# Hybrid decoder block on one core: another order of the second product's seven products, early scaling at its end, and three smaller edits

## The chip, the cores and the metric

The kernel runs on one core of one Trainium2 chip. Its engines are TensorE (PE, matmuls; its weight loads are PEld), VectorE (DVE), ScalarE (ACT), GpSimd (POOL) and SyncE (SP, which issues nearly all transfers). The metric is the device time of one execution in microseconds (us), the median of several.

## The reference

A decoder block over 512 positions of 2048 features, all in float32: eight heads of causal attention with forget gates and eight heads of spatial gating, both from one input projection, an output projection, and a dense layer with squared ReLU between 2048 and 8192 features; a norm ahead of each part and one at the end.

```python
h = rmsnorm(x, norm_mix_g);  z = h @ w_in           # q, k, v, log_f, zu, zv
attn = forgetting_attention(q, k, v, log_sigmoid(z_f + b_f))
gm = chunked_spatial_gating(zu, zv, gmlp_ln_g, gmlp_ln_b, w_s, b_s)
merged = concat(rmsnorm(attn, attn_out_g), rmsnorm(gm, gmlp_out_g))
x = x + merged @ w_out
a = relu(rmsnorm(x, norm_ffn_g) @ w_ff1)
x = x + (a * a) @ w_ff2
return rmsnorm(x, norm_final_g)
```

## The kernel before

Every large product is done with float32 numbers split into a high and a low part: of each tile ScalarE casts the high part (`wh`), VectorE subtracts it for the low part (`wl`), and TensorE does three matmuls (high by high, high by low, low by high). TensorE's instructions stand in the order in which the code is written; those of the other engines are placed by a scheduler, which keeps what their data need.

*Input and output units.* Up to 527 us units of 16 weight tiles make v, qk, zv and zu, with the attention heads' small matmuls between them; the units `oa` (attention's half of the output projection, to 605 us) and `og` (the gated half, to 703 us) follow. Behind each head, ScalarE copies the head's output out of PSUM, POOL squares it and adds the squares up (L429 to L433). The attention's norm `rA` is applied when an `oa` unit ends: VectorE multiplies the PSUM tile by `rA`, POOL adds the block's input `x4` (L600, L601). In `attn_split_task` (L442) the attention's output is cast and split.

*Block sums for the first product.* Beside these units, `sums_task` (L673) loads three blocks of `w_ff1` per step, adds two pairs (L680, L681) and stores both sums, in four steps of the task's clock.

*The first product* (703 to 1353 us) and *the second* (1353 to 1984 us) use seven block products in place of eight. The second has 16 units, eight slices of the hidden features (`kc`) by two halves of the output (`n`). A unit has products P1 to P7, each of two groups (`h`) of 12 matmuls 128x512. The tuple `usual` is the order of the products in a unit; `final` that of the last unit. Four blocks of `w_ff2` (B11, B12, B21, B22) are loaded per unit and half; `prepare` (L880), two groups ahead of the matmuls, forms the block sum that a product needs in place (B11 += B12 for P5, B11 += B22 for P6, B12 += B22 for P7, B21 += B11 beside P6), splits it, and where a block has had its last reader (`follows`) loads the next unit's.

The products accumulate in three pairs of PSUM banks: P1, P6, P7 and P4 in X, P2 in Y, P5 and P3 in Z. P7 goes on in the banks that hold P6, P4 in those of P7; P1, P6 and P5 are copied out by ScalarE when they end (`keep`, L916), and the outputs `acc` add up on VectorE: the PSUM tile (L924, or L909 for P4) and the copy (L925). Unit by unit:

```python
usual = (P1, P2, P5, P6, P7, P3, P4)
final = (P1, P2, P5, P6, P3, P7, P4)
follows = {P6: B11, P7: B12, P3: B22, P4: B21}
```

*The end.* In the last two units (`kc` is `LAST`) each finished output tile is scaled by the second norm's `r2` and added to the residual `x2` (`settle`, L957), and ScalarE squares it with a running sum. `finish` (L961), once per half of the positions, takes the root (`rl`), scales `acc` on VectorE and ScalarE (L972, L970), transposes it on TensorE (L981), multiplies by the last norm's columns, half of each PSUM tile on VectorE and half on ScalarE (L988, L990), and stores 512 KB per piece (L991).

## Time and profile before

| | |
|---|---|
| Median of 3 runs | 2000.34 us (1999.61 to 2003.0) |
| Profiled execution | 2002.97 us, of which the span 2001.3 us |
| Mean granted clock of TensorE | 0.998 |
| TensorE busy | 1966.3 us, 98% |
| VectorE busy | 1597.4 us, 80% |
| ScalarE busy | 1051.7 us, 53% |
| POOL busy | 84.1 us, 4% |
| Mean DMA traffic | 220 GB/s |

The span runs from the first to the last instruction of the profiled execution; the reported time has 1.7 us more around it. Busy time is the union of an engine's instructions. Matmuls overlap and their ends are modelled, so a delay of a fraction of a microsecond need not show as idle time: the distance of the starts tells more. A row of the timeline joins alike instructions that follow one another; "[1.62 <-ACT wh L895]" at its end says that the engine sat idle for 1.62 us before it, until ScalarE's `wh` of line 895 was there.

### The profile page before, as it was taken

To read this page: it belongs to the slowest core of one execution; us is meant where nothing else is said; L and a number is where in the kernel's file an instruction comes from. 1 tells how busy PE (TensorE), PEld (TensorE's weight loads), DVE (VectorE), ACT (ScalarE), POOL (GpSimd) and SP (SyncE) were. 2 spreads that over 40 slices of the span, in tenths; PEclk is the share of its full clock that TensorE was granted. 3 is DMA by queue.
4 is the path that set the end of the run, shared out by engine and by line. 5 is a ranking of instruction groups with operands and counts; after the bars stand their busy time and mean duration, and the time that the engine had idled before them with its cause. 6 is when DMAs were issued, how large, how long until landed. Compare 5 with 4: busy or idle time off the path is not lost.

```text
span 2001.3 us, 30641 instructions
## 1 busy us (share of the span) xinstructions
PE 1966.3 (98%) x11288; PEld 1721.9 (86%) x11288; DVE 1597.4 (80%) x2400; ACT 1051.7 (53%) x1692; POOL 84.1 (4%) x84
## 2 busy tenths in 40 slices
PE   9999999999999999999999999999999999999996
PEld 6888887888787899999999999997888888888875
DVE  7567567677667789888888888888888988998897
ACT  6344334445423566666666666666554444444455
POOL 5000001100121000000000000000000000000000
PEclk9999999999999999999999999999999999999999
DMA  6465565667766789986677667778855656646632
GB/s 217 152 198 167 186 193 174 200 211 242 247 204 199 249 270 307 334 270 201 207 243 238 209 203 236 240 263 314 328 198 202 231 165 224 241 137 237 245 128 84
DMA packets 226406, 439.91 MB, mean 220 GB/s; under 512 B 18896, under 2 KB 96848, under 8 KB 226128
## 3 DMA queue, kind: packets, MB, share of 16 engines
q1 hardware_dynamic: 225568, 436.09, 64.6%
q8 instruction: 88, 1.44, 0.3%
q10 hardware_dynamic: 432, 1.35, 0.2%
q0 software_dynamic: 256, 0.52, 0.1%
q14 instruction: 62, 0.51, 0.1%
HBM read 337.22 MB, written 100.66 MB: 219 GB/s over the span
## 4 chain that ended last, share of the span: by engine, by line
PE 58%; DVE 5%; DMA 3%; issue 1%; ACT 1%; SPq 0%; POOLq 0%; POOL 0%; DVEq 0%; ACTq 0%
PE q L802 28%; PE bX L1078 16%; PE bZ L1078 7%; PE bY L1078 4%; DMA b<-in_w_dram 1%; DVE wl L896 1%; PE ps_og L152 1%; PE ps_og L150 1%; PE ps_og L151 1%; DVE fl L734 1%; DMA x2d<-x2t 1%; DMA x2l<-x2d 0%; DVE acc L957 0%; DVE acc L924 0%; DMA t1d<-b 0%
## 5 line engine op out<-in xcount | busy, mean ns | idle before, releaser
L802 PE MATMUL q<-form,fh 128*128 128x256 f32 x3584 | 647.4, 283 | 1.0 <-DVE x L616 1.0
L802 PEld LDWEIGHTS q<-form,fh 128*128 128x128 f32 x3584 | 559.4, 192 | 1.4 <-DVE x L616 1.0
L802 PE MATMUL q<-form,fl 128*128 128x256 f32 x1792 | 508.6, 284 | 2.1 <-DVE fl L734 1.9
L895 ACT CAST wh<-raw 128x1024 fp32r<-128x1024 f32 x224 | 234.4, 1054 | 221.4 <-PE bX L1078 121.3
L802 PEld LDWEIGHTS q<-form,fl 128*128 128x128 f32 x1792 | 343.9, 192 | 4.1 <-DVE fl L734 3.4
L896 DVE TENSOR_TENSOR wl<-raw,wh 128x1024 fp32r<-128x1024 f32 x224 | 271.2, 1223 | 72.6 <-ACT wh L895 71.7
L1078 PE MATMUL bX<-wh,fac 128*128 128x512 f32 x1008 | 322.3, 393 | 4.3 <-ACT k_wl L916 2.1
L1078 PEld LDWEIGHTS bX<-wh,fac 128*128 128x128 f32 x1008 | 190.0, 188 | 52.3 <-ACT k_wh L916 6.8
L734 DVE TENSOR_TENSOR fl<-t,fh 128x512 fp32r<-128x512 f32 x256 | 176.2, 690 | 68.0 <-ACT fh L733 66.8
L733 ACT CAST fh<-t 128x512 fp32r<-128x512 f32 x256 | 158.2, 618 | 117.0 <-PE q L802 78.8
L1078 PE MATMUL bX<-wl,fac 128*128 128x512 f32 x504 | 198.8, 394 | 1.9 <-DVE wl L896 1.9
L1078 PE MATMUL bZ<-wh,fac 128*128 128x512 f32 x512 | 162.8, 389 | 0.0
L1078 PEld LDWEIGHTS bX<-wl,fac 128*128 128x128 f32 x504 | 95.0, 188 | 25.5 <-DVE wl L896 7.0
L1078 PEld LDWEIGHTS bZ<-wh,fac 128*128 128x128 f32 x512 | 96.1, 188 | 20.0
L733 ACT CAST fh<-r 128x512 fp32r<-128x512 f32 x128 | 79.1, 618 | 46.0 <-PE q L802 39.9
L150 PE MATMUL ps_qk<-xh,wh_qk 128*128 128x512 f32 x256 | 101.6, 397 | 0.0
L152 PE MATMUL ps_qk<-xh,wl_qk 128*128 128x512 f32 x256 | 100.0, 391 | 0.0
L151 PE MATMUL ps_qk<-xl,wh_qk 128*128 128x512 f32 x256 | 99.8, 390 | 0.0
L1078 PE MATMUL bZ<-wl,fac 128*128 128x512 f32 x256 | 99.6, 389 | 0.0
L734 DVE TENSOR_TENSOR fl<-r,fh 128x512 fp32r<-128x512 f32 x128 | 88.2, 689 | 10.1 <-ACT fh L733 9.4
L162 ACT ACTIVATE wh_qk<-raw_qk,cols 128x512 fp32r<-128x512 f32 x64 | 46.3, 724 | 94.7 <-PE ps_qk L151 62.9
L163 DVE SCALAR_TENSOR_TENSOR wl_qk<-raw_qk,cols,wh_qk 128x512 fp32r<-128x512 f32 x64 | 47.7, 750 | 59.0 <-ACT wh_qk L162 58.9
(618 smaller groups left out, 3559.1 us busy)
## 6 DMA issues: line engine op xcount, KB each, us to landing
b<-in_w_dram SPq DMA_DIRECT2D x256, 256.0 KB, 4.4
raw<-in_w_dram SPq DMA_DIRECT2D x128, 512.0 KB, 4.9
fac<-fac SPq DMA_DIRECT2D x112, 512.0 KB, 6.3
r<-in_w_dram SPq DMA_DIRECT2D x64, 512.0 KB, 5.6
fac<-fc SPq DMA_DIRECT2D x48, 512.0 KB, 3.9
raw_qk<-in_win_dram SPq DMA_DIRECT2D x32, 512.0 KB, 3.8
t1d<-b SPq DMA_DIRECT2D x64, 256.0 KB, 2.2
t3d<-b SPq DMA_DIRECT2D x64, 256.0 KB, 2.4
```

Of the source, the lines that this page charges most:

```text
L150: nc.tensor.matmul(ps, lhsT=ah, rhs=bh, start=start, stop=False)
L151: nc.tensor.matmul(ps, lhsT=ah, rhs=bl, start=False, stop=False)
L152: nc.tensor.matmul(ps, lhsT=al, rhs=bh, start=False, stop=stop)
L162: nc.scalar.activation(wh, raw, AF.Copy, scale=g)
L163: nc.vector.scalar_tensor_tensor(wl, raw, g, f(wh), ALU.mult, ALU.subtract)
L733: nc.scalar.copy(pairs(wh), b[p])
L734: nc.vector.tensor_tensor(pairs(wl), b[p], pairs(f(wh)), ALU.subtract)
L802: nc.tensor.matmul(d, lhsT=l[:, c], rhs=r, start=j == 0 and q == 0 and m == 0 and w == 0, stop=j == 3 and q == 1 and w == 2, skip_group_ch ...
L895: nc.scalar.copy(wh, s)
L896: nc.vector.tensor_tensor(wl, s, f(wh), ALU.subtract)
L1078: nc.tensor.matmul(banks[chain][t], lhsT=l, rhs=r, start=start and w == 0, stop=stop and w == 2, skip_group_check=True)
```

## The change

There are five edits.

1. The second product's order becomes P1, P5, P6, P2, P7, P3, P4, so P2 stands between P6 and P7; B21 += B11 moves from P6 to P2, and the next unit's B11 is loaded behind P2.
2. The scaling by `r2` and the residual come early: `settle_task` turns each `acc` into acc * r2 + x2 at the start of the last slice, and the additions of the last two units become scaled additions (`add_scaled`, with `nr2`, the negative of `r2`, for subtractions). Squares have a function of their own; the very last one is VectorE's.
3. In `finish` VectorE scales five of eight tiles and ScalarE three; the transposed tiles use two more PSUM banks, each tile is read by one engine, and the last piece of each half is stored in two parts of 256 KB.
4. `sums_task` does one block sum per step of its clock, with one store behind each.
5. The attention's squares go from POOL to ScalarE; the multiplication by `rA` moves from the end of the `oa` units to `attn_split_task`; the end of an `oa` unit is one addition on VectorE, and POOL's sixteen additions there are gone.

```diff
@@ attention head, split, end of an oa unit
-            nc.gpsimd.tensor_tensor(attnT["ss"], a, a, ALU.mult)
+            nc.scalar.activation(attnT["ss"], a, AF.Square)
...
-            nc.gpsimd.tensor_tensor(sq, a, a, ALU.mult)
+            nc.scalar.activation(sq, a, AF.Square)
             nc.gpsimd.tensor_tensor(attnT["ss"], attnT["ss"], sq, ALU.add)
...
+                nc.vector.tensor_tensor(attnT[c][:, j, :], attnT[c][:, j, :], rA, ALU.mult)
                 nc.scalar.copy(attn_h[c][:, j, :], attnT[c][:, j, :])
...
-                nc.vector.tensor_tensor(o, ps[m], rA, ALU.mult)
-                nc.gpsimd.tensor_tensor(o, o, x4[c][:, m, :], ALU.add)
+                nc.vector.tensor_tensor(o, ps[m], x4[c][:, m, :], ALU.add)
@@ sums_task
                 here(nc.vector.tensor_tensor(b11, b11, b12, ALU.add))
+                yield 1
+                here(nc.sync.dma_start(out=t1d[u][j], in_=b11))
                 here(nc.vector.tensor_tensor(b22, b22, b12, ALU.add))
                 yield 1
-                here(nc.sync.dma_start(out=t1d[u][j], in_=b11))
                 here(nc.sync.dma_start(out=t3d[u][j], in_=b22))
-                yield 1
@@ second product
-    usual = (P1, P2, P5, P6, P7, P3, P4)
+    usual = (P1, P5, P6, P2, P7, P3, P4)
-        final = (P1, P2, P5, P6, P3, P7, P4)
+        final = (P1, P5, P6, P2, P3, P7, P4)
-        follows = {P6: B11, P7: B12, P3: B22, P4: B21}
+        follows = {P2: B11, P7: B12, P3: B22, P4: B21}
...
-            if p == P6:
+            if p == P2:
                 nc.vector.tensor_tensor(raw(B21), raw(B21), raw(B11), ALU.add)
@@ its end
+                if end:
+                    add_scaled(c, t, bank[t], ps_op)
+                    add_scaled(c, t, s[t], s_op)
...
+        def settle_task(n):
+            order = ((0, 2 * n), (0, 2 * n + 1), (1, 2 * n + 1), (1, 2 * n))
+            x2 = {c: load_x2(*c) for c in order}
+            yield 3
+            for c in order:
+                for t in range(2):
+                    a, tb = acc[c][:, t, :], 2 * c[0] + t
+                    nc.vector.scalar_tensor_tensor(a, a, r2[:, tb:tb + 1], x2[c][:, t, :], ALU.mult, ALU.add)
+                yield 1
+
+        def add_scaled(c, t, src, op):
+            a, tb = acc[c][:, t, :], 2 * c[0] + t
+            r = (nr2 if op is ALU.subtract else r2)[:, tb:tb + 1]
+            nc.vector.scalar_tensor_tensor(a, src, r, a, ALU.mult, ALU.add)
...
+            if kc == LAST and p == P1 and h == 0:
+                start_task(settle_task(n))
@@ finish
-                    if t:
+                    if t and q < 3:
                         nc.scalar.activation(a, a, AF.Copy, scale=rt)
...
-                    ps = mm(f"pt{th}{q}{jj}")
+                    i = 2 * q + jj
+                    ps = ax(f"pt{th}{i}", i // 2 % 2) if i % 2 else mm(f"pt{th}{i}")
...
+                    if i in ((1, 2, 4, 6, 7) if th else (0, 2, 4)):
+                        nc.vector.tensor_tensor(d, ps.rearrange("p (j c) -> p j c", j=2),
+                                                cols[:, G_LAST + k:G_LAST + k + 2].unsqueeze(2).broadcast_to([P, 2, 256]),
+                                                ALU.mult)
+                    else:
+                        for j in range(2):
+                            nc.scalar.activation(d[:, j, :], ps[:, j * 256:(j + 1) * 256], AF.Copy,
+                                                 scale=cols[:, G_LAST + k + j:G_LAST + k + j + 1])
+                    if jj or q == 3:
+                        m = slice(0, 4) if q < 3 else slice(2 * jj, 2 * jj + 2)
```

How the change moves the other engines' instructions is seen at three places. ScalarE in unit 6, a steady unit of the second product; `wh6_6_1` is the high part for P6's second half, `k5` the copy of P5, `k2` that of P6, `bX` and `bZ` the PSUM banks. Before:

```order
L895 CAST wh6_5_0_17139<-raw6_0_0_16889 128x1024
L895 CAST wh6_5_1_17158<-raw6_0_1_16911 128x1024
L895 CAST wh6_6_0_17179<-raw6_0_0_16889 128x1024
L916 COPY k5_6_wh_17220<-bZ6_0_17186 128x512
L916 COPY k5_6_wl_17221<-bZ6_1_17187 128x512
L895 CAST wh6_6_1_17201<-raw6_0_1_16911 128x1024
L895 CAST wh6_7_0_17225<-raw6_1_0_16937 128x1024
L895 CAST wh6_7_1_17244<-raw6_1_1_16956 128x1024
L916 COPY k2_6_wh_17262<-bX6_0_17104 128x512
L916 COPY k2_6_wl_17263<-bX6_1_17105 128x512
```

After the change:

```order
L895 CAST wh6_5_0_17094<-raw6_0_0_16883 128x1024
L895 CAST wh6_5_1_17113<-raw6_0_1_16902 128x1024
L916 COPY k1_6_wh_17129<-bX6_0_17098 128x512
L916 COPY k1_6_wl_17130<-bX6_1_17099 128x512
L895 CAST wh6_6_0_17134<-raw6_0_0_16883 128x1024
L895 CAST wh6_6_1_17153<-raw6_0_1_16902 128x1024
L916 COPY k5_6_wh_17169<-bZ6_0_17138 128x512
L916 COPY k5_6_wl_17170<-bZ6_1_17139 128x512
L895 CAST wh6_2_0_17173<-raw6_2_0_17017 128x1024
L895 CAST wh6_2_1_17192<-raw6_2_1_17035 128x1024
L916 COPY k2_6_wh_17211<-bX6_0_17098 128x512
L916 COPY k2_6_wl_17212<-bX6_1_17099 128x512
```

Both casts for P6 now stand ahead of the copies of P5 rather than around them, and the casts for P2 stand between the copies of P5 and those of P6.

VectorE in the same unit, from P5's low part on (`raw6_0` is B11, `raw6_1` B12, `raw6_2` B21, `raw6_3` B22). Before:

```order
L896 TENSOR_TENSOR wl6_5_0_17140<-raw6_0_0_16889,wh6_5_0_17139 128x1024
L889 TENSOR_TENSOR raw6_0_0_16889<-raw6_0_0_16889,raw6_3_0_16981 128x1024
L896 TENSOR_TENSOR wl6_5_1_17159<-raw6_0_1_16911,wh6_5_1_17158 128x1024
L924 TENSOR_TENSOR acc00_15277<-acc00_15277,bY6_0_17143 128x512
L924 TENSOR_TENSOR acc00_15277<-acc00_15277,bY6_1_17144 128x512
L925 TENSOR_TENSOR acc00_15277<-acc00_15277,k1_6_wh_17134 128x512
L925 TENSOR_TENSOR acc00_15277<-acc00_15277,k1_6_wl_17135 128x512
L896 TENSOR_TENSOR wl6_6_0_17180<-raw6_0_0_16889,wh6_6_0_17179 128x1024
L898 TENSOR_TENSOR raw6_2_0_17024<-raw6_2_0_17024,raw6_0_0_16889 128x1024
L889 TENSOR_TENSOR raw6_0_1_16911<-raw6_0_1_16911,raw6_3_1_16999 128x1024
L898 TENSOR_TENSOR raw6_2_1_17042<-raw6_2_1_17042,raw6_0_1_16911 128x1024
L896 TENSOR_TENSOR wl6_6_1_17202<-raw6_0_1_16911,wh6_6_1_17201 128x1024
```

After the change:

```order
L887 TENSOR_TENSOR raw6_0_0_16883<-raw6_0_0_16883,raw6_1_0_16928 128x1024
L896 TENSOR_TENSOR wl6_1_1_17073<-raw6_0_1_16902,wh6_1_1_17072 128x1024
L909 TENSOR_TENSOR acc12_15275<-acc12_15275,bX5_0_16797 128x512
L909 TENSOR_TENSOR acc12_15275<-acc12_15275,bX5_1_16798 128x512
L896 TENSOR_TENSOR wl6_5_0_17095<-raw6_0_0_16883,wh6_5_0_17094 128x1024
L887 TENSOR_TENSOR raw6_0_1_16902<-raw6_0_1_16902,raw6_1_1_16949 128x1024
L889 TENSOR_TENSOR raw6_0_0_16883<-raw6_0_0_16883,raw6_3_0_16974 128x1024
L891 TENSOR_TENSOR raw6_1_0_16928<-raw6_1_0_16928,raw6_3_0_16974 128x1024
L896 TENSOR_TENSOR wl6_5_1_17114<-raw6_0_1_16902,wh6_5_1_17113 128x1024
L896 TENSOR_TENSOR wl6_6_0_17135<-raw6_0_0_16883,wh6_6_0_17134 128x1024
L889 TENSOR_TENSOR raw6_0_1_16902<-raw6_0_1_16902,raw6_3_1_16992 128x1024
L891 TENSOR_TENSOR raw6_1_1_16949<-raw6_1_1_16949,raw6_3_1_16992 128x1024
```

The additions of P4 of unit 5 (L909) are followed at once by P5's low part and the block sums; P2's low parts and B21's sums, which stood ahead, come last.

VectorE at the end of the first `oa` unit (`b910` and `b912` are block sums of the first product, `u1` the gated part). Before:

```order
L600 TENSOR_TENSOR oa0_4912<-ps_oa0_0_4705,rA_144 128x512
L600 TENSOR_TENSOR oa0_4912<-ps_oa0_1_4706,rA_144 128x512
L600 TENSOR_TENSOR oa0_4912<-ps_oa0_2_4707,rA_144 128x512
L600 TENSOR_TENSOR oa0_4912<-ps_oa0_3_4708,rA_144 128x512
L680 TENSOR_TENSOR b910_4846<-b910_4846,b911_4847 128x512
L681 TENSOR_TENSOR b912_4848<-b912_4848,b911_4847 128x512
L163 SCALAR_TENSOR_TENSOR wl_oa1_3_4924<-raw_oa1_2_4894,cols_112,wh_oa1_3_4923 128x512
L163 SCALAR_TENSOR_TENSOR wl_oa1_4_4954<-raw_oa1_4_4951,cols_112,wh_oa1_4_4953 128x512
L534 SCALAR_TENSOR_TENSOR u1_4678<-pm6_4945,cols_112,u1_4678 128x4x128
```

After the change:

```order
L601 TENSOR_TENSOR oa0_4920<-ps_oa0_0_4710,x4_0_4704 128x512
L601 TENSOR_TENSOR oa0_4920<-ps_oa0_1_4711,x4_0_4704 128x512
L601 TENSOR_TENSOR oa0_4920<-ps_oa0_2_4712,x4_0_4704 128x512
L601 TENSOR_TENSOR oa0_4920<-ps_oa0_3_4713,x4_0_4704 128x512
L680 TENSOR_TENSOR b910_4854<-b910_4854,b911_4855 128x512
L163 SCALAR_TENSOR_TENSOR wl_oa1_3_4927<-raw_oa1_2_4902,cols_112,wh_oa1_3_4926 128x512
L683 TENSOR_TENSOR b912_4856<-b912_4856,b911_4855 128x512
L163 SCALAR_TENSOR_TENSOR wl_oa1_4_4957<-raw_oa1_4_4954,cols_112,wh_oa1_4_4956 128x512
L535 SCALAR_TENSOR_TENSOR u1_4683<-pm6_4948,cols_112,u1_4683 128x4x128
```

The four rows of the unit's end read `x4` in place of `rA`, and the two block sums, which stood together, now have a low part of the next weights between them.

## Rows read from the trace of the kernel before

**Rows 1.** Page, part 1: busy us, share of the span, instructions by engine.

```profile
PE 1966.3 (98%) x11288; PEld 1721.9 (86%) x11288; DVE 1597.4 (80%) x2400; ACT 1051.7 (53%) x1692; POOL 84.1 (4%) x84
```

**Rows 2.** Timeline, TensorE: start us, duration, instruction; idle before and releaser.

```profile
541.99 0.47 PE L150 MATMUL pm<-gvh,wsh 128*128 128x512 f32 x1 [1.38 <-DVE u L534]
...
1378.60 0.50 PE L1078 MATMUL bX<-wh,fac 128*128 128x512 f32 x1 [2.11 <-ACT k_wl L916]
...
1919.14 0.50 PE L1078 MATMUL bX<-wl,fac 128*128 128x512 f32 x1 [0.77 <-DVE wl L896]
...
1956.53 0.49 PE L1078 MATMUL bX<-wh,fac 128*128 128x512 f32 x1 [1.62 <-ACT wh L895]
...
1958.12 0.50 PE L1078 MATMUL bX<-wl,fac 128*128 128x512 f32 x1 [1.09 <-DVE wl L896]
...
1979.83 1.25 PE L981 MATMUL pt<-ident,acc 128*128 128x128 f32 x8 [1.72 <-DVE acc L909]
```

**Rows 3.** Waits of TensorE: us in total, times, longest.

```profile
PE pS L150 <- DVE mx L382: 3.9, 4, 1.4
```

**Rows 4.** Timeline, TensorE, in a steady unit of the second product.

```profile
1608.33 0.61 PE L1078 MATMUL bX<-wh,fac 128*128 128x512 f32 x2
...
1609.22 0.63 PE L1078 MATMUL bX<-wh,fac 128*128 128x512 f32 x2
...
1610.61 0.62 PE L1078 MATMUL bX<-wh,fac 128*128 128x512 f32 x2
...
1611.29 0.89 PE L1078 MATMUL bX<-wh,fac 128*128 128x512 f32 x2
...
1612.26 0.63 PE L1078 MATMUL bX<-wh,fac 128*128 128x512 f32 x2
```

**Rows 5.** Timeline, ScalarE: unit 0, the steady unit, the end.

```profile
1377.96 0.58 ACT L916 COPY k_wl<-bX 128x512 f32<-128x512 f32 x1
...
1606.52 2.00 ACT L895 CAST wh<-raw 128x1024 fp32r<-128x1024 f32 x2
...
1611.04 0.59 ACT L916 COPY k_wh<-bX 128x512 f32<-128x512 f32 x1 [1.17 <-PE bX L1078]
...
1988.55 2.56 ACT L970 ACTIVATE acc<-acc,rl 128x512 f32<-128x512 f32 x4 [1.23 <-POOL rl L123]
```

**Rows 6.** Timeline, VectorE: early part, unit 0, P4's additions, the end.

```profile
535.58 1.53 DVE L680 TENSOR_TENSOR b<-b,b 128x512 f32<-128x512 f32 x1
...
1383.02 1.23 DVE L896 TENSOR_TENSOR wl<-raw,wh 128x1024 fp32r<-128x1024 f32 x1 [2.27 <-ACT wh L895]
...
1473.78 1.28 DVE L909 TENSOR_TENSOR acc<-acc,bX 128x512 f32<-128x512 f32 x2
...
1607.61 3.52 DVE L896 TENSOR_TENSOR wl<-raw,wh 128x1024 fp32r<-128x1024 f32 x3 [0.20 <-ACT wh L895]
...
1898.93 1.28 DVE L909 TENSOR_TENSOR acc<-acc,bX 128x512 f32<-128x512 f32 x2
...
1988.55 1.67 DVE L972 TENSOR_SCALAR acc<-acc,rl 128x512 f32<-128x512 f32 x4 [0.81 <-POOL rl L123]
1991.51 3.23 DVE L988 TENSOR_SCALAR y<-pt,cols 128x256 f32<-128x256 f32 x8 [1.28 <-ACT y L990]
```

**Rows 7.** DMA issues: count, KB each, median us from issue to landing.

```profile
raw<-in_w_dram SPq DMA_DIRECT2D x128, 512.0 KB, 4.9
...
t1d<-b SPq DMA_DIRECT2D x64, 256.0 KB, 2.2
...
out_dram<-y SPq DMA_DIRECT2D x8, 512.0 KB, 3.8
```

**Rows 8.** Windows, TensorE: span, us; busy (instructions), granted clock, DMA share, GB/s.

```profile
1380.40:1383.20 2.80, 2.80 (x8) 0.52 0.89 288
```

**Rows 9.** Lines, VectorE: busy us, mean ns, idle before.

```profile
L957 DVE SCALAR_TENSOR_TENSOR acc<-acc,r,x2l 128x512 f32<-128x512 f32 x16 | 11.3, 746 | 0.0
```

**Rows 10.** Lines, POOL: busy us, mean ns, idle before.

```profile
L601 POOL TENSOR_TENSOR oa<-oa,x 128x512 f32<-128x512 f32 x12 | 17.9, 1523 | 55.8 <-issue 40.0 <-DVE oa L600 15.8
```

More of the change, by code (lines that the diff above doesn't have):

```diff
@@ L917, in keep, with add_kept @@
             return s, how
-        def add_kept(c, s, first, bank, ps_op, s_op):
+        def add_kept(c, s, first, end, bank, ps_op, s_op):
             for t in range(2):
                 a = acc[c][:, t, :]
-                if not first:
+                if end:
+                    add_scaled(c, t, bank[t], ps_op)
+                    add_scaled(c, t, s[t], s_op)
+                elif not first:
                     nc.vector.tensor_tensor(a, a, bank[t], ps_op)
@@ L933, in second_product @@
         rl = const.tile([P, NT], F32, name="rl")
+        nr2 = sm.tile([P, NT], F32, tag="rt", name="nr2")
         def load_x2(th, q):
@@ L951, in second_norm, with squares @@
             nc.vector.tensor_tensor(r2, r2, r2, ALU.mult)
-        def settle(th, q, x2l):
-            a = acc[th, q]
-            for t in range(2):
-                tb = 2 * th + t
-                nc.vector.scalar_tensor_tensor(a[:, t, :], a[:, t, :], r2[:, tb:tb + 1], x2l[:, t, :],
-                                               ALU.mult, ALU.add)
-                nc.scalar.activation(x2l[:, t, :], a[:, t, :], AF.Square, accum_out=sums[:, tb, q:q + 1])
+            nc.vector.tensor_scalar(nr2, r2, -1.0, None, ALU.mult)
+        def settle_task(n):
[11 more added lines that the diff above has]
+            nc.vector.scalar_tensor_tensor(a, src, r, a, ALU.mult, ALU.add)
+        def squares(c, t, eng=None):
+            a = acc[c][:, t, :]
+            s = sums[:, 2 * c[0] + t, c[1]:c[1] + 1]
+            junk = w_pool.tile([P, 512], F32, tag="wl", name=f"junk{c[0]}{c[1]}{t}")
+            if eng is nc.vector:
+                nc.vector.tensor_tensor_reduce(junk, a, a, 1.0, 0.0, ALU.mult, ALU.add, accum_out=s)
+            else:
+                nc.scalar.activation(junk, a, AF.Square, accum_out=s)
         def finish(th):
@@ L982, in finish @@
                                                 acc[th, q][:, t, c * P:(c + 1) * P], ident)
[L983 to L992 removed]
+                    k = 4 * q + 2 * jj
+                    d = y[:, 2 * jj:2 * jj + 2, :]
+                    if i in ((1, 2, 4, 6, 7) if th else (0, 2, 4)):
+                        nc.vector.tensor_tensor(d, ps.rearrange("p (j c) -> p j c", j=2),
+                                                cols[:, G_LAST + k:G_LAST + k + 2].unsqueeze(2).broadcast_to([P, 2, 256]),
+                                                ALU.mult)
+                    else:
+                        for j in range(2):
[3 more added lines that the diff above has]
+                        m = slice(0, 4) if q < 3 else slice(2 * jj, 2 * jj + 2)
+                        nc.sync.dma_start(out=out[q * 512 + m.start * P:q * 512 + m.stop * P,
+                                                  th * 256:(th + 1) * 256].rearrange("(m p) c -> p m c", p=P),
+                                          in_=y[:, m, :])
                 if q == 1:
@@ L1007, in done @@
                 if end:
-                    settle(*c, x2_for[c])
+                    for t in range(2):
+                        squares(c, t)
             if p == P1:
@@ L1012, in evacuate @@
                 take(X, how)
-                if end:
-                    for c in ((0, lo), (0, hi), (1, hi), (1, lo)):
-                        x2_for[c] = load_x2(*c)
             elif p == P2:
-                add_kept((0, lo), kept[1], first, Y, ALU.add, ALU.add)
+                add_kept((0, lo), kept[1], first, end, Y, ALU.add, ALU.add)
                 done((0, lo))
@@ L1025, in evacuate @@
             elif p == P7:
-                add_kept((1, hi), kept[5], first, X, ALU.subtract, ALU.add)
+                add_kept((1, hi), kept[5], first, end, X, ALU.subtract, ALU.add)
                 if o is final:
-                    take(X, add_ps((1, lo)))
+                    for t in range(2):
+                        add_scaled((1, lo), t, X[t], ALU.add)
                 done((1, hi))
             elif p == P3:
-                add_kept((0, hi), kept[2], first, Z, ALU.add, ALU.subtract)
+                add_kept((0, hi), kept[2], first, end, Z, ALU.add, ALU.subtract)
                 done((0, hi))
@@ L1035, in evacuate @@
             elif p == P4:
-                b = banks["W"] if o is final else X
                 if first:
-                    take(b, lambda t, ps: nc.scalar.copy(acc[1, lo][:, t, :], ps))
-                else:
-                    take(b, add_ps((1, lo)))
-                done((1, lo))
+                    take(X, lambda t, ps: nc.scalar.copy(acc[1, lo][:, t, :], ps))
+                elif end:
+                    b = banks["W"] if o is final else X
+                    for t in range(2):
+                        add_scaled((1, lo), t, b[t], ALU.add)
+                        squares((1, lo), t, nc.vector if o is final and t else None)
+                else:
+                    take(X, add_ps((1, lo)))
                 if o is final:
                     start_task(finish(1), 1)
-        x2_for = {}
-        for p, b in ((P1, B11), (P2, B21), (P5, B12), (P6, B22)):
+        for p, b in ((P1, B11), (P5, B12), (P6, B22), (P2, B21)):
             load_factor(0, p)
```

16 lines of the change are left out of this document (5 added, 11 removed).

## The prediction, made before the change was run

> **What bounds the kernel now.** I read the page's first part, then the gaps of TensorE in the timeline, then the starts of its matmuls inside one unit of the second product, then ScalarE and VectorE at those places, and last the end. TensorE is busy 1966.3 us of a span of 2001.3 [rows 1], and the change adds and removes no matmul, so it can only win idle time, late matmuls and the end. Span less busy is 35 us. The gaps that the change touches are in [rows 2]: 1.38 at 541.99, in the early part; 2.11 early in the second product; 0.77, 1.62 and 1.09 in its last two units; 1.72 near the end. The attention scores wait four times, 3.9 us, on VectorE's maximum [rows 3].
>
> More is lost where the profile shows no gap. Three matmuls of 512 columns take 0.68 us from start to start (1610.61 to 1611.29) [rows 4]. In the unit shown the step from 1608.33 to 1609.22 is 0.89, and that from 1611.29 to 1612.26 is 0.97: 0.21 and 0.29 late, 0.5 us per unit. The first is P6's second half, whose low part waits: ScalarE cast its high part only after the two copies of P5 (casts from 1606.52) [rows 5]. The second is P7, which accumulates in the banks that P6 has just left: ScalarE starts to copy them out at 1611.04 [rows 5], one tile after the other, and P7's matmuls for the second bank cannot start before. It recurs: VectorE's addition of P4 comes at 1473.78 and, eleven units later, at 1898.93 [rows 6], 38.65 us per unit, where 168 matmuls (56 steps of 0.68) need 38.08. So each steady unit holds 0.5 to 0.57 us.
>
> **The second product's order.** P2, in its own banks, now stands between P6 and P7: ScalarE's copies of P6 get two groups, 5.44 us, in place of none, so P7's 0.29 goes. In the new list of ScalarE both casts of P6 stand ahead of the copies of P5, so the 0.21 goes too. Gain 0.5 us in each of the units 1 to 13: **6.5 us**.
>
> Can something new be late? Block sums for P5 and P6 are now wanted two groups sooner. From the start of a unit VectorE has to do, in the new order, two additions of P4 (1.28 for the pair, 0.6 from one to the next [rows 6]), then 1.14 per full tile (three take 3.52 at 1607.61, the last one's drain of 0.1 included [rows 6]): the low part of P5, three block sums, P5's second low part. That ends at 0.1 + 1.3 + 5 x 1.14 = 7.1 us; it is wanted at 8.16 + 0.23. P6's follow at 8.3 and 11.7, wanted at 11.1 and 13.8. Slack 1.3 us at the tightest place. The cover is that VectorE works some 33.4 us of 38.08 per unit: 22 full tiles x 1.14 + 14 additions x 0.6. If ScalarE is late by more than 1.3 us at P5, the excess is lost again in every unit. The reload of each block changes to four positions, 21.8 us, where B21 had 10.9, against a landing of 4.9 us [rows 7]; nothing there.
>
> **The units at the ends of the second product.** In unit 0 P7 waited 2.11 for a copy that ScalarE started at 1377.96, behind casts of the first product's last results [rows 5]; right after it the granted clock was 0.52 from 1380.4 to 1383.2, the lower level of 1.2 GHz [rows 8], where 2.8 x 0.48 = 1.3 us of work was lost. With the unit's own 0.5 that is 3.9 us. All of this falls, as P7 is no longer next. But P5 is now second, and VectorE is still adding up the first product then (the row at 1383.02 shows it waiting 2.27 for a cast that unit 0's crowded ScalarE made late [rows 6]): P6 may be up to 1.8 us late, and if the clock falls again, 1.3 more. Between 0 and 3.1 I take 1.4: **2.5 us**.
>
> Units 14 and 15 lost 0.77, 1.62 and 1.09 [rows 2] beside their late matmuls of 0.5, 4.5 us in all. VectorE there scales sixteen accumulator tiles by 0.746 us [rows 9] on top of its 33.4 us: eight per unit, 39 of 38.08. The early scaling has the same sixteen, but the scheduler puts two in unit 12, seven in 13, six in 14, one in 15, and the additions of the last two units become the slower form, 14 x 0.07 = 1 us each. Unit 13: 33.4 + 7 x 0.67 = 38.1, unit 14 38.4. Moreover in units 13 to 15 both halves' first block sums stand ahead of P5's low part: 0.1 + 1.3 + 4 x 1.14 = 6.0 us, wanted at 5.67; about 0.4 lost there, 0.2 more at P6. Between 0.6 and 4 us for the three units I take 2: **2.5 us**.
>
> **The end.** Of the first half's transposes one lot waits 1.72 for VectorE to empty a bank that P4 shares [rows 2]; with the transposed tiles spread over four banks it doesn't. At the very end both engines scale from 1988.55 on, VectorE copies out its last eight tiles from 1991.51 for 3.23 us [rows 6], and the span ends 6.5 us behind. ScalarE's four scalings are the longer arm (2.56 [rows 5] against 1.67 [rows 6]); with three and five both take about 2: 0.4 us. The last store, 512 KB at a median of 3.8 us, becomes 256 KB; the nearest row for that size is 2.2 us [rows 7], so up to 1.6; I take 1.4. The Trainium skill, page DMA: Bandwidth & Descriptors, section Anatomy of one DMA, gives (for transfers that GpSimd issues) a fixed 2 us plus size over 436 GB/s, by which halving would give an estimated 0.6 and the sum would be 0.8 us smaller. Against it stands VectorE: it has five more scaled additions in the way between P4's last matmul and the sum of squares, and takes one of ScalarE's squares; I charge 1.0. 1.7 + 0.4 + 1.4 - 1.0: **2.5 us**, bounds 0 and 4.5.
>
> **The early part.** At 535.58 a block sum takes 1.53 us [rows 6] beside POOL's additions (1.52 each [rows 10]), where additions of that size take 0.64 (the pairs of [rows 6]); the next sum stands beside them too, so VectorE is some 1.8 us late there. POOL's sixteen additions, 17.9 us in the larger group of twelve [rows 10], go, VectorE does one addition in place of a multiplication, and the second sum now stands behind a low part that the matmuls want. 1.8 is more than the 1.38 at 541.99 [rows 2], so that gap goes. The eight multiplications moved into the split cost VectorE 8 x 0.64 = 5 us, in the last of the input units, where TensorE waits for nothing; without that room it would be late by one tile, 0.6 us. The attention scores' waits, 3.9 us [rows 3]: in some a sum now comes before the mask and one behind it, not two in front. Between 0 and 2.5 I take 0.3 beyond the 1.4: **1.7 us**. The eight squares on ScalarE follow a copy there, and it is busy 53% [rows 1].
>
> **Sum.** 6.5 + 2.5 + 2.5 + 2.5 + 1.7 = 15.7 us. The profiled execution took 2002.97 (span 2001.3 and 1.7 around it), so the changed kernel's should take 1987.3; the median of the runs shown is 2.6 us lower, 2000.34, so I forecast 1984.7, **1985 us**.
>
> **Rivals.** *Half gain:* the order works but VectorE, at 33.4 of 38.08 us, is late elsewhere, in unit 0, in 12 to 15, or in the end, where its backlog eats the 2.5 us. Then the 6.5 of the steady units and the 1.7 of the early part stay: 2000.3 - 8.2 = 1992 us. For it: VectorE is already the releaser in the last units; against it: 4.7 us of room per steady unit. Chance 0.18.
> *No change:* the slack of 1.3 us at P5 is spent, since ScalarE's cast follows a block sum and precedes the low part, so 0.5 us per unit goes from P6 to P5; end and early part give 2.5 + 1.7 at most: 1997 us. Chance 0.07.
> *Slower:* the same chain, block sum, cast, low part, at P5. Lateness beyond the 7.1 reckoned above costs nothing up to 1.3 us, and up to 1.8 it is no worse than today's 0.5; from there on every unit loses. At the 2.27 us that VectorE waited for one cast in unit 0 [rows 6] the price is 16 x (2.27 - 1.8) = 7.5 us, the gains of units 0, 14 and 15 are gone, and VectorE's backlog takes the end's too; 1.7 of the early part are left: 2000.3 + 7.5 - 1.7 = 2006 us. Against it: in the steady unit VectorE's waits for casts are 0.2 at that place of the timeline, and ScalarE has half its time free. Chance 0.04.
> *Better:* nothing new is late: 6.5 + 3.9 + 4.5 + 4.5 + 3.9 = 23 us: 1977. Chance 0.10.
> The forecast, within 1981 to 1990, holds 0.61.
>
> **Range and chances.** A measurement can tell about 0.2%, 4 us, from no change: faster is below 1996.3. The range goes from 1978 to 1996, which leaves out the slower case, most of the no-change one and half of the best, under 2 in 10. Faster 0.88, same 0.08, slower 0.04.
>
> **What would show it.** In the profile after: the step between VectorE's additions of P4, 38.65 now, should be 38.1; no wait on ScalarE's copies in the second product; granted clock 1.00 throughout 1370 to 1400; POOL's busy time down by some 33 us from 84.1, and no gap at the matmul behind 541; at the end less than 8.1 us from the last transpose to the end. Wrong it would be if steps of 38.3 or more stayed in the middle units (then a low part of P5 or P6 is the releaser), or if units 12 to 15 showed gaps of over 3 us in sum behind VectorE's scaling.

## The result and the profile after

The changed kernel takes 1980.53 us (median of 4 runs, 1978.56 to 1981.12) against 1999.97 (4 runs, 1998.4 to 2003.0) of the kernel before: 0.9898 of its time, 95% interval 0.9886 to 0.9911, 19.4 us less. The forecast was 1985, range 1978 to 1996.

The profiled execution took 1980.68 us, span 1977.7 (so 3.0 us stand around the span, where the profile of before had 1.7), granted clock 0.999. Part 1 of the page after:

```profile
PE 1957.2 (99%) x11288; PEld 1723.5 (87%) x11288; DVE 1589.7 (80%) x2405; ACT 1054.5 (53%) x1696; POOL 50.2 (3%) x60
```

TensorE is 99% busy, and POOL's time fell by 33.9 us [rows 1]. The longest waits of TensorE after the change (us in total, times, longest):

```profile
PE pt L1008 <- DVE acc L994: 2.9, 1, 2.9
PE pS L150 <- DVE mx L382: 2.6, 4, 1.2
PE q L802 <- DVE fl L734: 2.2, 5, 0.8
```

No wait of the second product is in this list, where [rows 2] had 2.11, 0.77, 1.62 and 1.09; in the whole of it TensorE has no idle time of over 0.15 us. The gap at the matmul behind 541 is gone too. The waits of the attention scores went from 3.9 [rows 3] to 2.6.

The timeline of TensorE after, in a steady unit: P5's second half (bZ), the start of P6's second half, and the step from P2 (bY) into P7 (L1114 is the old L1078):

```profile
1586.70 0.39 PE L1114 MATMUL bZ<-wl,fac 128*128 128x512 f32 x1
...
1591.69 0.61 PE L1114 MATMUL bX<-wh,fac 128*128 128x512 f32 x2
...
1592.37 0.61 PE L1114 MATMUL bX<-wh,fac 128*128 128x512 f32 x2
...
1599.85 0.39 PE L1114 MATMUL bY<-wh,fac 128*128 128x512 f32 x1
...
1600.53 0.61 PE L1114 MATMUL bX<-wh,fac 128*128 128x512 f32 x2
```

Every step of three matmuls is 0.68 us, in P6 (1591.69 to 1592.37) as at the start of P7 (1599.85 to 1600.53), where [rows 4] had 0.89 and 0.97. VectorE after, the addition of P4 in two units three apart, and behind the later one that unit's second low part of P5 with the first of P6:

```profile
1464.27 1.28 DVE L909 TENSOR_TENSOR acc<-acc,bX 128x512 f32<-128x512 f32 x2
...
1578.51 1.28 DVE L909 TENSOR_TENSOR acc<-acc,bX 128x512 f32<-128x512 f32 x2
...
1584.25 2.50 DVE L896 TENSOR_TENSOR wl<-raw,wh 128x1024 fp32r<-128x1024 f32 x2
```

From 1464.27 to 1578.51 a unit takes 38.08 us, against 38.65 [rows 6]; that is 56 steps of 0.68, so nothing is late in these units. By the starts of the matmuls a little lateness is left where no gap shows: 0.3 us in unit 0, 0.3 in each of the units 13 and 14, 0.6 in unit 15. The low part that starts at 1584.25 runs about 1.2 us, to 1585.5; its first matmul starts at 1586.70, 1.2 us later. ScalarE after, in the same unit:

```profile
1587.99 1.05 ACT L895 CAST wh<-raw 128x1024 fp32r<-128x1024 f32 x1 [2.50 <-DVE raw L889]
1588.95 0.58 ACT L916 COPY k_wh<-bZ 128x512 f32<-128x512 f32 x1
...
1594.15 0.59 ACT L916 COPY k_wh<-bX 128x512 f32<-128x512 f32 x1 [0.94 <-PE bX L1114]
```

The casts for P6 (the last starts at 1587.99) come ahead of the copies of P5 at 1588.95. The copies of P6's banks start at 1594.15, six us before P7's matmuls want the banks (from 1600.07), where [rows 5] had 1611.04 and matmuls waiting at 1611.29. The clock after, where [rows 8] had 0.52 (windows of TensorE: length, busy, granted clock, DMA share, GB/s):

```profile
1372.00:1380.00 8.00, 8.00 (x37) 1.00 0.96 337
1380.00:1390.00 10.00, 10.00 (x46) 1.00 0.89 322
```

The end, TensorE before and after, then VectorE after:

```profile
1977.07 1.04 PE L981 MATMUL pt<-ident,acc 128*128 128x128 f32 x8
...
1989.09 4.05 PE L981 MATMUL pt<-ident,acc 128*128 128x128 f32 x32 [3.50 <-DVE acc L972]
```

```profile
1957.60 1.91 PE L1008 MATMUL pt<-ident,acc 128*128 128x128 f32 x16
1959.27 0.48 PE L1114 MATMUL bW<-wh,fac 128*128 128x512 f32 x1
...
1962.12 1.91 PE L1008 MATMUL pt<-ident,acc 128*128 128x128 f32 x16
1966.96 3.84 PE L1008 MATMUL pt<-ident,acc 128*128 128x128 f32 x32 [2.93 <-DVE acc L994]
```

```profile
1966.42 2.07 DVE L994 TENSOR_SCALAR acc<-acc,rl 128x512 f32<-128x512 f32 x5 [0.81 <-POOL rl L123]
1968.40 3.28 DVE L1014 TENSOR_TENSOR y<-pt,cols 128x512 f32<-128x512 f32 x5
```

The matmuls of the last product's second half begin at 1959.27, 1.7 us after the transposes that stand ahead of them; before, it was 3.8 us (1977.07 to 1980.83), with a wait of 1.72 among those transposes [rows 2]. VectorE's scaling starts at 1966.42 and goes on without a pause into its copies, where before it stood idle for 1.28 us until ScalarE's first copy [rows 6]. Its last copy ends at 1971.68; the span ends 6.0 us later, against 6.5 before [rows 6]. The stores of the output, and the DMA traffic while the last of them land, after and before (its last two numbers are DMA share and GB/s):

```profile
out_dram<-y SPq DMA_DIRECT2D x6, 512.0 KB, 3.5
out_dram<-y SPq DMA_DIRECT2D x4, 256.0 KB, 3.7
```

```profile
1970.70:1975.70 5.00, 0.10 (x1) 0.71 1.03 340
```

```profile
1994.30:1999.30 5.00, 0.00 (x0) 0.82 1.03 343
```

A part of 256 KB landed in 3.7 us, the whole pieces in 3.5; [rows 7] had 3.8 for whole pieces. From shortly before the last copy's end until two us before the span's, the stores move 340 GB/s, after as before. The last store after the change is issued at 1972.65 and lands at 1976.73, 0.8 us behind the one ahead of it, which landed at 1975.97: it stands in line.

One more difference at the end isn't in the list of edits: the second half's output tiles `y` have buffers of another pool than before (`raw_pool`).

### The profile page after: what moved, and what is told of

It is laid out like the page before. It is cut to its first block, busy times and chain, and to the rows that moved or that the text cites. A ratio compares the mean times of both kernels' runs of the same rounds, so it can differ in the third digit from the quotient of the medians.

```text
span 1977.7 us, 30578 instructions
## 1 busy us (share of the span) xinstructions
PE 1957.2 (99%) x11288; PEld 1723.5 (87%) x11288; DVE 1589.7 (80%) x2405; ACT 1054.5 (53%) x1696; POOL 50.2 (3%) x60
## 4 chain that ended last, share of the span: by engine, by line
PE 62%; DVE 2%; DMA 1%; issue 1%; ACT 0%; SPq 0%; DVEq 0%; POOLq 0%; POOL 0%; ACTq 0%
PE q L802 30%; PE bX L1114 17%; PE bZ L1114 8%; PE bY L1114 4%; PE ps_og L152 1%; PE ps_og L151 1%; PE ps_og L150 1%; DMA b<-in_w_dram 1%; DMA t1d<-b 1%; DVE wl L896 0%; DVE acc L972 0%; DVE fl L734 0%; PE px L646 0%; PE pt L1008 0%; ACT wh L895 0%
## 5 line engine op out<-in xcount | busy, mean ns | idle before, releaser
L1114 PE MATMUL bX<-wh,fac 128*128 128x512 f32 x1008 | 318.1, 389 | 0.0
L1114 PEld LDWEIGHTS bX<-wh,fac 128*128 128x128 f32 x1008 | 189.2, 188 | 39.2
L1114 PE MATMUL bX<-wl,fac 128*128 128x512 f32 x504 | 196.5, 390 | 0.0
L1114 PE MATMUL bZ<-wh,fac 128*128 128x512 f32 x512 | 162.8, 389 | 0.0
L1114 PEld LDWEIGHTS bZ<-wh,fac 128*128 128x128 f32 x512 | 96.1, 188 | 19.9
L1114 PEld LDWEIGHTS bX<-wl,fac 128*128 128x128 f32 x504 | 94.6, 188 | 21.1 <-DVE wl L896 1.5
L1114 PE MATMUL bZ<-wl,fac 128*128 128x512 f32 x256 | 99.8, 390 | 0.1
```

The source lines that it names most:

```text
L1114: nc.tensor.matmul(banks[chain][t], lhsT=l, rhs=r, start=start and w == 0, stop=stop and w == 2, skip_group_check=True)
```

## The experiments

All times are medians; every set of runs had its own runs of the kernel before beside it: 2000.99 us in the first set (the four kernels with other orders), 2001.48 in the second (two more operations, the sums, the attention, the store), 2002.13 in the third (one more operation, the sums in pairs, the changed kernel again), 1999.78 in the last (two banks). Ratios are to those. "Late" is what the starts of matmuls lie apart beyond 0.68 us for each step of three.

**The order alone.** The kernel before with the first edit:

```diff
-    usual = (P1, P2, P5, P6, P7, P3, P4)
+    usual = (P1, P5, P6, P2, P7, P3, P4)
-        final = (P1, P2, P5, P6, P3, P7, P4)
+        final = (P1, P5, P6, P2, P3, P7, P4)
```

(with the block sum, the reloads and the first loads that go with it)

> The kernel before with the second product's new order alone. Theory: the order by itself takes away the late matmuls of the steady units (0.5 us each), the 2.11 us wait of unit 0 and the drop of the clock behind it, while the end and the early part stay as they were and the scaling still crowds the last two units: about 11 us less than before, 1989 (1987 to 1991), steps of 38.1 us between VectorE's additions of P4. Rival: the early scaling carries most of the gain in the second product; then this kernel stays above 1994.

Measured: 1990.15 us, ratio 0.9942 (0.9926 to 0.9959), 10.8 us less. The middle units have no late matmul left. Its gaps in the second product are 0.28 in unit 1 and, in the last unit, these two of TensorE's timeline, at P5:

```profile
1930.73 0.50 PE L1078 MATMUL bZ<-wh,fac 128*128 128x512 f32 x1 [0.94 <-ACT wh L895]
1932.48 0.79 PE L1078 MATMUL bZ<-wl,fac 128*128 128x512 f32 x1 [1.25 <-DVE wl L896]
```

So the order carries the steady units and unit 0, as the theory had it. The old scaling in the last unit keeps 2.2 us of gaps; by the starts the unit is 4.4 us late at the end of its P5, and the granted clock from 1932 to 1934 was 0.50.

**All but the order.** The changed kernel with the order of before. In the last two units P2's addition then stands ahead of the scaling of its tile, so the values of those tiles are not the reference's; the instructions are as many.

```diff
-    usual = (P1, P5, P6, P2, P7, P3, P4)
+    usual = (P1, P2, P5, P6, P7, P3, P4)
```

> The changed kernel with the old order of the second product, all else changed. Theory: the gains of the early part (4 us) and the end (4 us) stay, and part of the gaps of the last two units; the late matmuls and unit 0's wait come back: 1991 (1989 to 1993), steps of 38.65. Rival, by which the early scaling carries the second product's gain: under 1987.

Measured: 1998.37, ratio 0.9984 (0.9975 to 0.9994), 2.6 us less, where I expected about 10. TensorE's gaps in the timeline:

```profile
1376.56 0.50 PE L1114 MATMUL bX<-wh,fac 128*128 128x512 f32 x1 [2.11 <-ACT k_wl L916]
...
1873.70 0.50 PE L1114 MATMUL bX<-wl,fac 128*128 128x512 f32 x1 [1.02 <-DVE wl L896]
...
1916.16 0.49 PE L1114 MATMUL bX<-wh,fac 128*128 128x512 f32 x1 [0.59 <-ACT wh L895]
1917.96 0.80 PE L1114 MATMUL bX<-wl,fac 128*128 128x512 f32 x1 [1.31 <-DVE wl L896]
```

The wait of unit 0 is back, 2.11 us as before (this time the granted clock behind it stayed at 1.00). The early part and the end keep their gains, 2.0 and 4.0 us in the profile. But the early scaling, which in the new order is harmless, makes gaps of 1.02, 0.59 and 1.31 in the units 13 and 14 in the old one, and more in unit 15, all behind the casts and low parts of P6. In the old order P6's second half is late in every unit, so VectorE has no slack there, and what the scaling adds is lost: the units 13 to 15, up to the transposes, take 3.1 us more than in the kernel before. There, early scaling is a gain in the new order alone.

**One cause or two: P6 and P7 as neighbours.** The kernel before with P2 between P5 and P6:

```diff
-    usual = (P1, P2, P5, P6, P7, P3, P4)
+    usual = (P1, P5, P2, P6, P7, P3, P4)
```

> The kernel before with the order P1, P5, P2, P6, P7, P3, P4 in the units but the last: P6 and P7 stay neighbours in one pair of banks, but P2 stands between P5 and P6, so that ScalarE's casts for P6 come behind the copies of P5 with a product to spare. Theory of two causes: P6's second half is on time (step of 0.68), P7's step of 0.97 and unit 0's wait stay; steps of 38.4 us per unit, 3 us less in all, 1997 (1995 to 1999). Rival, one cause (ScalarE's order of casts alone): steps of 38.1 and 1992.

Measured: 1996.35, ratio 0.9974 (0.9964 to 0.9984), 4.6 us less. TensorE in a steady unit, and VectorE's addition of P4 in two units:

```profile
1602.97 0.62 PE L1078 MATMUL bX<-wh,fac 128*128 128x512 f32 x2
...
1604.33 0.62 PE L1078 MATMUL bX<-wh,fac 128*128 128x512 f32 x2
...
1605.01 0.89 PE L1078 MATMUL bX<-wh,fac 128*128 128x512 f32 x2
...
1605.98 0.63 PE L1078 MATMUL bX<-wh,fac 128*128 128x512 f32 x2
...
1583.68 0.68 DVE L909 TENSOR_TENSOR acc<-acc,bX 128x512 f32<-128x512 f32 x1
...
1622.10 1.28 DVE L909 TENSOR_TENSOR acc<-acc,bX 128x512 f32<-128x512 f32 x2
```

P6's steps are 0.68 throughout, while P7's first step (1605.01 to 1605.98) stays 0.97; the unit takes 38.42 us. Two causes, as the theory said: of the 0.57 us per unit the casts' place among ScalarE's copies is worth 0.23 (38.65 to 38.42), the neighbouring banks 0.34 (38.42 to 38.08). Two things I had not expected: unit 0 waits 0.6 and 0.2 us at P7 in place of 2.11 and is 3.0 us shorter than before, and the last unit, whose own order is the old one, is 2.9 us longer up to the transposes.

**P3 between P6 and P7.** The kernel before with this order, and B22 reloaded behind P7:

```diff
-    usual = (P1, P2, P5, P6, P7, P3, P4)
+    usual = (P1, P2, P5, P6, P3, P7, P4)
```

> The kernel before with the order P1, P2, P5, P6, P3, P7, P4 in all units: P3, in other banks, stands between P6 and P7, while ScalarE's copies of P5 still stand between the casts of P6. Theory of two causes: P7 is on time, P6's second half stays 0.2 late; steps of 38.35, unit 0's wait and the clock's drop are gone: 0.3 x 13 + 3.4 = 7 us less, 1993 (1991 to 1995). Rival, one cause (the casts' order): steps of 38.6 in spite of P3, 1997 or more. Second rival, one cause (the banks): steps of 38.1, 1990.

Measured: 2004.36, ratio 1.0014 (1.0004 to 1.0023): 3.4 us more, where I expected 7 less. TensorE at P4 of a unit, and VectorE's addition of P4 in two units:

```profile
1501.99 0.47 PE L1079 MATMUL bX<-wh,fac 128*128 128x512 f32 x1 [0.38 <-DVE acc L925]
...
1624.05 1.28 DVE L910 TENSOR_TENSOR acc<-acc,bX 128x512 f32<-128x512 f32 x2
...
1663.01 1.28 DVE L910 TENSOR_TENSOR acc<-acc,bX 128x512 f32<-128x512 f32 x2
```

The units take 38.96 us, more than before. P7 is on time and P6's second half stays 0.24 late, as the theory of two causes had it; P4 is now 0.63 late in each unit. Now P4 follows P7 in the same banks, and VectorE, which takes P7 out with two additions per bank, releases them later than ScalarE did with one copy. I had overlooked this neighbour. It tells the same rule from the other side: a product that goes on in the banks of the one right before it waits for its reader, 0.34 us if that is one copy per bank, 0.63 if it is two additions.

**The slack at P5.** The changed kernel with n further VectorE operations per unit ahead of P5's second low part, n = 1 and 2:

```diff
+            if p == P5 and h == 1:
+                for _ in range(n):
+                    nc.vector.tensor_tensor(wl, s, s, ALU.subtract)
             nc.scalar.copy(wh, s)
```

With one:

> The changed kernel with one more VectorE operation of a full tile (1.14 us) ahead of P5's second low part in every unit, written to the tile that the low part goes to just after. With the slack of 1.3 us nothing of it is seen in the steady units: matmul steps of 0.68 and 38.1 us per unit; in units 13 to 15, which have less room, up to 1 us each: 1982 (1980 to 1984). Rival, a slack half as large: 0.6 us in each unit, 1990.

Measured: 1987.5, ratio 0.9930 (0.9915 to 0.9944), 6.2 us more than the changed kernel of its set and 3.5 above the range that I gave. TensorE's waits on low parts:

```profile
PE bZ L1117 <- DVE wl L899: 2.4, 5, 1.0
...
PE bX L1117 <- DVE wl L899: 1.5, 1, 1.5
```

These six waits, 3.9 us, lie in the units 0, 1 and 13 to 15; the units 2 to 12 show none. By the starts, though, the units 3 to 12 are 0.11 to 0.13 us late at P5's second half (38.2 us per unit). So the slack of the steady units is about 1.0 us, 1.14 less 0.12, and not the 1.3 reckoned; units 0 and 1 have none to spare, which I had not expected. With two:

> The changed kernel with two more VectorE operations of a full tile (1.14 us each) ahead of P5's second low part in every unit; they write to the tile that the low part is written to just after. My reckoning of the slack: the low part ended at 7.1 us after the unit's start and was wanted at 8.4; here eight tiles stand before its end (the scheduler lets P6's first low part go ahead), 1.4 + 8 x 1.14 = 10.5, so TensorE waits 2.1 us in each of 16 units: 34 us more, 2014 (2005 to 2020). Rival: only the sum of VectorE's work per unit counts (4.7 us of room); then 1981 to 1984.

Measured: 2023.34, ratio 1.0111 (1.0096 to 1.0126), 43 us more than the changed kernel where 34 were reckoned, 3 above the range that I gave, and 22 slower than before:

```profile
PE bZ L1117 <- DVE wl L899: 31.8, 16, 2.7
```

16 waits, one per unit, at the low part of P5: 0.3 and 0.4 us in the units 2 and 1, 2.07 to 2.70 in the others, 2.0 in the mean, close to the 2.1 reckoned. The starts lie some 0.3 us further apart than the gaps say, and a part of the rest is the lower granted clock that follows five of them (0.61 in the four us behind the gap at 1480.39): those units are some 4 us late, their neighbours 2.4. The rival, by which only VectorE's work per unit counts, is out: VectorE had room, and the place decided.

**One block sum per step.** The kernel before with the fourth edit alone (one `yield` between the two sums, the first store behind it):

> The kernel before with one block sum per step of the task's clock, nothing else. Theory: the attention scores' waits shrink by about 1 us of 3.9, and the gap of 1.4 at the gated part's mix falls in part, since the second slowed sum stands behind a low part: 1.5 us less, 1998.5 (1997 to 2000). Rival: the gain of 4 us in the early part comes wholly from POOL's adds that went; then no change here.

Measured: 2002.86, ratio 1.0009 (0.9999 to 1.0018): no gain, where I expected 1.5. The waits of the scores are 4.1 us, five of them, and the gap of 1.4 at the gated part stays. In the first product there are late low parts that the kernel before has not:

```profile
829.34 0.39 PE L802 MATMUL q<-form,fl 128*128 128x256 f32 x1 [1.27 <-DVE fl L734]
...
832.94 0.39 PE L802 MATMUL q<-form,fl 128*128 128x256 f32 x1 [0.47 <-DVE fl L734]
```

**The attention's edits alone.** The kernel before with the squares on ScalarE, `rA` at the split and one addition at the end of an `oa` unit:

> The kernel before with the attention's edits alone (squares on ScalarE, the norm applied at the split, one addition on VectorE at the end of an output unit). Theory: the gap of 1.4 us goes, and with the squares off POOL the waits of the scores shrink by 0.5 to 1: 2.5 us less, 1997.5 (1996 to 1999). Rival: the early gain is that of the sums; then at most 1 us here.

Measured: 1998.08, ratio 0.9982 (0.9973 to 0.9992), 3.4 us less. The gap at 541.99 is gone, the scores wait 3.0 us, and POOL has this left of the attention (busy, mean ns):

```profile
L433 POOL TENSOR_TENSOR ssa<-ssa,sqa 128x512 f32<-128x512 f32 x7 | 9.0, 1288 | 260.3 <-ACT sqa L432 260.3
```

So the early gain is that of these edits. Over all profiles it is clearest at the first matmul of the first product: in the five kernels with the old attention it starts between 696.45 and 698.50, in the nine with the new one between 694.62 and 695.99; the means are 2.5 us apart.

**The sums in pairs again.** The changed kernel without the fourth edit, beside the changed kernel itself:

> The changed kernel with the block sums in pairs again, as before. Theory: the split of the pairs gave nothing in the early part and brought late low parts in the first product near 790, 826 and 830 us (1.9 us together in the profile after), in exchange for one of 0.7 near 720: about 1 us less than the changed kernel, 1979.5 (1978 to 1981). Rival, by the prediction: the attention scores' waits come back, 0.3 to 1 us more.

> The changed kernel once more, beside the others of this set: 1980.5 (1978.5 to 1982.5). Its profile shows how far the early part, 4.0 us shorter in the first profile, varies by itself: theory 1 to 2 us, so that the second product begins between 1349 and 1351.5.

Measured: 1981.6 (ratio 0.9897, 0.9882 to 0.9912) and 1981.29 (0.9893, 0.9877 to 0.9910): no difference that can be told, where I expected about 1 us. TensorE's wait on the first product's low parts, first with the sums in pairs, then in the changed kernel:

```profile
PE q L802 <- DVE fl L734: 0.9, 2, 0.6
```

```profile
PE q L802 <- DVE fl L734: 3.2, 6, 1.4
```

The 2.3 us that are won here are partly lost at the scores (3.2 against 2.8 us), and the rest is less than the times can tell. The profiles side by side can: from its first matmul to that of the second product, the first product takes 653.4 to 655.0 us in the six kernels with the sums in pairs (mean 654.0) and 654.4 to 656.2 in the eight with one sum per step (mean 655.2). The late low parts between 824 and 833 are in all eight and in none of the six. So the fourth edit costs some 1.2 us in the mean. In its second profile the changed kernel begins the second product at 1351.77, 2.3 us later than in the first and just above the range that I gave.

**The last store in one piece.** The changed kernel with `if jj:` in place of `if jj or q == 3:`, and whole pieces:

> The changed kernel with the last piece of each half stored in one transfer of 512 KB, as before. By the prediction's term (256 KB land 1.4 us sooner): 1.4 us more, 1982. Rival, by the profile after, where the parts of 256 KB took 3.7 us and the whole pieces 3.5: within 0.5 us of the changed kernel.

Measured: 1982.64, ratio 0.9906 (0.9889 to 0.9922), its interval over that of the changed kernel: the median is 1.4 and 2.1 us above the changed kernel's two, but the runs of before beside the three differ by as much, so the times do not decide between the term and its rival. In the profile the span ended 5.5 us after VectorE's last copy (which ends at 1975.63, of a span of 1981.1), against 6.0 with the parts; but the last transposes ran at a lower clock here (5.16 us), and where the changed kernel's did too (5.50, see the last section) it ended 4.9 us after that copy. From the first transpose to the end of the span it is 20.9 us, against 20.1 and 20.6 in the changed kernel's two profiles. So the last part's size is worth 0.2 to 0.8 us by the profiles, and not 1.4.

**Two banks for the transposes.** The changed kernel with

```diff
-                    ps = ax(f"pt{th}{i}", i // 2 % 2) if i % 2 else mm(f"pt{th}{i}")
+                    ps = mm(f"pt{th}{i}")
```

> The changed kernel with the transposed tiles in the pair of banks of the matmuls' pool alone, as before; who reads them, the scaled additions and the rest of the end stay. By the prediction's term of 1.7 us for the wait of the transposes on VectorE: the step into the last product's second half grows from 1.7 us in the profile after back to some 3.5, and this kernel takes 1982.5 to 1984. Rival: VectorE is no longer behind at that place, since the scaling went from the end, and the four banks are worth nothing: 1980.5 to 1981.5.

Measured: 1984.63, ratio 0.9922 (0.9906 to 0.9939). TensorE at the end:

```profile
1959.04 1.03 PE L1008 MATMUL pt<-ident,acc 128*128 128x128 f32 x8
1962.26 1.17 PE L1008 MATMUL pt<-ident,acc 128*128 128x128 f32 x8 [2.18 <-DVE acc L972]
1963.18 0.49 PE L1114 MATMUL bW<-wh,fac 128*128 128x512 f32 x1
...
1970.03 5.17 PE L1008 MATMUL pt<-ident,acc 128*128 128x128 f32 x29 [2.07 <-DVE acc L994]
```

The wait among the first half's transposes is back, 2.18 us, and the last product's second half begins 4.1 us behind the first transposes instead of 1.7. Some of it returns, as the last wait is 2.1 in place of 2.9: from the first transpose to the first of the last 32 it is 11.0 us (1959.04 to 1970.03) against 9.4 (1957.60 to 1966.96). The spread over four banks is worth 1.6 us there. At the end of the span 1.4 are left, against the changed kernel's second profile, whose last 32 transposes took the same 5.50 us (22.0 and 20.6 us from the first transpose). The median is 3.3 to 4.1 us above the changed kernel's two and 0.6 above the range that I gave; what it is longer beyond the 1.4 I don't put on the banks, and it stays open.

## Why the prediction was right

The time fell inside the range and near the forecast; the steps of the second product were right in their mechanisms and reckoned somewhat small. In the early part the sum came near by luck, since two terms were off in opposite directions; at the end, terms that were off both ways cancelled in part.

- *Steady units, 6.5 us.* 0.57 us per unit were won (38.65 to 38.08), 7.4 for the units 1 to 13 by the starts of the matmuls. Both causes are shown, by the kernel with P6 and P7 as neighbours and by the order alone.
- *New lateness at P5.* Reckoned end of the low part 7.1 us after the unit's start, slack 1.3. The profile shows 7.2 and 1.2; the kernel with one more operation shows that about 1.0 of it can be used, the one with two a wait of 2.0 for 2.1. The rivals that rested on this slack (no change, slower) were priced by the right mechanism: with two more operations the changed kernel is slower than before. (The sum of the no-change rival, 2000.3 less 4.2, is 1996.1 and not 1997, which changes nothing.)
- *Unit 0, 2.5 us.* Some 4: the wait of 2.11 and the low clock are gone, and P6 was 0.3 us late, not 1.4 (the upper bound of 1.8 had no row behind it). VectorE's tail of the first product cost nearly nothing, though the kernel with one more operation shows that it was close.
- *Units 14 and 15, 2.5 us.* Again some 4: the lateness charged to the early scaling, 2 for the units 13 to 15, is there at the places named but smaller. The profile has no gap; the starts are 0.25 us late at P6 in the units 13 and 14, and 0.40 at P5 and 0.23 at P6 in unit 15, 1.2 in all. The order alone leaves 2.2 us of gaps in the last unit, and the early scaling in the old order makes gaps; neither by itself gives this.
- *The end, 2.5 us.* From the first transpose to the end of the span it is 4.1 us less (24.2 to 20.1). The bank spread, 1.7, measured 1.4 to 1.6. The other scaling, 0.4, came with a gain that the prediction had not counted: from its start to VectorE's first copy it was 2.96 us [rows 6], now 1.98. VectorE's five scalings take 0.4 longer than four, but the 1.28 that it then stood idle behind ScalarE's first copy [rows 6] are gone; each tile now has one reader and `y` another pool, and which of the two did it was not tried. The last store, 1.4, measured 0.2 to 0.8: this term was sized too large. It took the landing time of the block sums' stores (2.2 us) for a part of that size, but behind the other stores the parts landed in 3.7. VectorE's backlog, charged at 1.0, didn't show: TensorE's wait before the last transposes fell from 3.50 to 2.93. So what the last store was too large by hid a part of what the other terms were short of.
- *The early part, 1.7 us.* The first profile shows 4.0: the second product begins at 1349.51 in place of 1353.50. That is not all the change: in the five kernels with the old attention it began between 1350.28 and 1353.50 (mean 1352.1), in the nine with the new one between 1348.78 and 1351.77 (mean 1350.2). The difference of the means is 1.9. Within the 1.7, the 1.4 of the gap at 541.99 came as reckoned, by the attention's edits, which win 2.5 us up to the start of the first product. The sums, to which I gave a share of the gain, have the other sign: they cost some 1.2 us in the first product. For the changed kernel's own pair of edits, the seven kernels that have both begin the second product at 1350.5 in the mean, the four that have neither at 1351.9: 1.4 us.

The spans of the two profiles differ by 23.6 us: the second product 15.5 by the starts of the matmuls, the end 4.1, the early part 4.0. Their times differ by 22.3, since 1.3 us more stand around the span after. With 1.4 for the early part the sum is 21.0, against 19.4 and 20.8 between the medians of two sets. What makes the early part vary from run to run stays open.

## What to carry to other kernels

Where products take turns in accumulation banks, put another bank's product between two that share one, and check the new neighbours as well: the reader with more work makes the longer wait. Idle columns of a profile don't show such waits when matmuls overlap; the distance between starts, or a unit's period over several units, does. Room is counted at the place where something is wanted, not over the unit: VectorE had 4.7 us free per unit, and about 1.0 that could be used at the tightest place.

## What the runs showed of the hardware

The last 32 transposes follow an idle time of 2.9 us of TensorE. They took 3.84 us in the profile after, and in the second run of the same kernel:

```profile
1969.32 5.50 PE L1008 MATMUL pt<-ident,acc 128*128 128x128 f32 x32 [2.94 <-DVE acc L994]
```

There the granted clock between 1971 and 1975 was 0.70, so for more than half of that time the lower level of 1.2 GHz:

```profile
1971.00:1975.00 4.00, 3.82 (x24) 0.70 0.67 224
```

The same gap, the same instructions, and 1.7 us between them by the clock's level; the kernel with the last store in one piece (5.16) and that with two banks (5.50) show it too. Of the 1.7 only 0.5 is left at the end of the span (20.1 and 20.6 us from the first transpose). So the ends of two single profiles can be compared to half a us at best, unless those transposes took alike. It is the same in the kernel with two more operations: after the same idle time of 2.07 us the granted clock of the next four us was 0.61 at 1480.39 and 1.00 at 1522.44.

The stores at the end moved at some 340 GB/s, and a part of 256 KB took as long (3.5 to 3.7 us in two profiles of the changed kernel) as the whole pieces of 512 KB (3.2 to 3.5). The Trainium skill's fixed-plus-size rule (page DMA: Bandwidth & Descriptors, section Anatomy of one DMA, stated there for transfers that GpSimd issues) would give an estimated 0.6 us for the half size; the landing times of these runs show none of it, the end of the span 0.2 to 0.8. A store's landing time is no fixed price here: of the block sums' two stores, of 256 KB too, the first took 2.2 us before [rows 7] and the second 2.4; with one sum per step the second takes 4.1:

```profile
t3d<-b SPq DMA_DIRECT2D x64, 256.0 KB, 4.1
```

Why it grew was not tried.
